# One more raw-weight buffer, one general slot and one residual slot fewer in a hybrid decoder layer

## The chip, the cores and the metric

The kernel runs on one core of one Trainium2 chip. The metric is the device time of one execution in microseconds (us), from launch to end. The span in the profile is a little shorter: it counts from the first to the last instruction.

## What is computed

One layer of a decoder trunk for 512 tokens of width 1024, in float32. Only the second half and the end of the first half matter for the change.

```python
u   = rms_norm(h, norm_mix_g)
z   = u @ w_in                                   # attention q/k/v, mLSTM inputs, gates ga, gb
m   = sigmoid(ga) * (ya @ w_proj_a) + sigmoid(gb) * (yb @ w_proj_b)
h   = h + m @ w_out                              # the first residual
u   = rms_norm(h, norm_ffn_g)
g, up = split(u @ w_gate_up)                     # 1024 x 5632
h   = h + (silu(g) * up) @ w_down                # 2816 x 1024, the second residual
out = rms_norm(h, norm_final_g)
```

Here `ya` is the output of a block-sparse attention and `yb` that of a chunkwise mLSTM; both are made from `z`.

## The kernel before

**Precision and weights.** TensorE takes operands in a float32 form of reduced precision. To keep the accuracy each operand is split into a high and a low half (`split_hl`, L157 to L162: ACT copies and rounds, DVE subtracts) and each product is three matmuls. So every weight tile passes through three places: a raw buffer that a DMA fills, ACT and DVE that split it, and two split tiles that PE reads.

**Buffers.** The pools are sized at L89 and L90. `NR` (tag R, 4 KB per partition) holds raw weights. `NW` (tag W, 4 KB, 10 of them) holds split halves and sums of weights. `NA` (tag A, 2 KB) holds everything general: activations, split halves of activations, gate tiles, outputs of a product on their way to DRAM. `NX` (tag X, 2 KB) holds the residual's input tiles `xr` and at the end the two tiles `g3` of the last norm's weights. `NR1` (tag R1) and `NA4` (tag A4) stay as they are. A tile takes a slot of its tag; the instruction that first writes it waits until the last reader of the slot's previous tile is done.

**Order.** Up to L1132 the order is written out by hand. Behind that a scheduler orders the instructions of each engine when the kernel is built, by priorities, by a model of times, and by slots that are free in that model; on the chip each engine and each queue takes its instructions in that fixed order. SP's queue carries nearly all loads; POOL's queue carries the accumulating DMAs.

**Front part (to some 404 us).** `UNITS` lists 60 weight tiles of 128 x 1024: q, k, va, ob, vb, qkb, ga, gb, then `p` (both projections) and `wo` (the output projection, eight units in the order `WO`). `load_pair` (L180) loads two raw tiles, `split_unit` (L189) splits them two units ahead of their use. Two tiles of the normalised input (`u`, L270) sit in the R pool as well, until the last unit that reads it, so this part has `NR` minus two raw buffers.

**Residual.** `load_xr` (L595) loads one tile of x on SP's queue: twice from `run_p`, then once in each `run_wo`. `run_wo` (L642) multiplies, adds the product into the `xr` tile (DVE, L651), and from the sum makes the operands `bq` of the gate-up products (L653 to L676). `residual` (L629) transposes the sum on PE (L635) one unit later and writes it to DRAM (`h1d`). An X slot is free when all of these have read it. `end_load` (L1063) puts `g3` into the same pool.

**Gate-up and down.** `ITEMS` lists 22 gate-up groups (`gu`), and after groups 4, 8, 12, 16 and 21 one down group (`ds`). Both use a Strassen-like scheme of seven products. `gu_load` (L688) loads for each group `w11` (R1) and two R tiles: `s13`, by a plain load on SP (L692) and an accumulating load on POOL (L693) that waits for the plain one, and `r` (L695). `ds_load` (L746) takes four R tiles (L750), the last one two more (L754). Loads are put in order with a look-ahead of three items (`load_next`, L1081). `gu_prep` (L722) makes sums and splits: S1 and S3 from `s13` (ACT L148, then DVE L731), S2 and S4 from `s24` (DVE L739, L740), and W12 and W22 from `r`. `gu_first`, `gu_main` and `gu_last` hold the products (`prod`, L777, whose three matmuls are L783 to L785); `ds_run` (L905) holds those of a down group (L894 to L896) and sends its results with accumulating DMAs on POOL's queue to `h1d` (L911).

Of the kernel before, what the change touches and what calls it, by code (L numbers as in the profile page):

```python
# [84 lines left out]
def hybrid_layer_kernel(ctx: ExitStack, tc, xT, wall, wgu, wds, wdl, g3v, vecs, wgates, consts, rope, out):  # L85
    nc = tc.nc
    V, A, T = nc.vector, nc.scalar, nc.tensor

    NA, NA4, NR, NR1, NW = 35, 7, 6, 3, 10  # L89
    NX = 3  # L90
    cst = ctx.enter_context(tc.tile_pool(name="cst", bufs=1))
    act = ctx.enter_context(tc.tile_pool(name="act", bufs=NA))
    sm = ctx.enter_context(tc.tile_pool(name="sm", bufs=6))
# [5 lines left out]
    def nm(p="t"):  # L99
        cnt[0] += 1  # L100
        return f"{p}{cnt[0]}"

    def slot(dt=F32, name="a"):
        return act.tile([P, S], dt, name=nm(name), tag="A")
# [490 lines left out]
    def load_xr():  # L595
        m = WO[len(xr)]
        t = act.tile([P, S], F32, name=nm("xr"), tag="X", bufs=NX)
        nc.sync.dma_start(t, xT[m])
# [464 lines left out]
    def end_load():  # L1063

        g3 = [act.tile([P, S], F32, name=nm("g3"), tag="X", bufs=NX) for _ in range(2)]
        hs = [[slot(name="h1") for _ in range(2)] for _ in range(4)]
# [519 lines left out]
```

## Time and profile before

| | us |
|---|---|
| median of 3 runs | 759.62 (758.28 to 760.0) |
| the profiled execution | 761.87 |
| its span | 760.1 |
| PE busy in it | 738.9 |
| DVE busy | 624.0 |
| ACT busy | 429.3 |
| DMA, mean over the span | 156 GB/s |

PE, TensorE's matmuls, is busy in 97% of the span; its weight loads run beside them. Matmuls overlap each other by their recorded durations, so the distance from one start to the next is the cost of one, not the duration in the row. The DMA engines' load is uneven: the page's slices go from 0 to over nine tenths and back in each period of the second part.

### The profile page before, as it was taken

The page shows a single profiled execution, that of the slowest core. Times are in us where ns is not written, and L with a number is a line of the kernel's source. Part 1 is how long each engine was busy: PE and PEld are TensorE (multiplying, and loading weights), DVE is VectorE, ACT ScalarE, POOL GpSimd, SP SyncE. Part 2 cuts the span into 40 slices and gives each one's busy share as a digit, 9 for nine tenths or more (in the row PEclk, how much of TensorE's full clock was granted, in tenths as well). Part 3 has the DMA queues.
Part 4 walks back from the last instruction along what each step waited for, and adds up shares of the span by engine and source line. Part 5 has one row for each costly group of instructions (what it writes and reads, how often), then busy time and mean ns, then how long its engine had stood idle before and what let it go on. Part 6 is the DMA issues. An engine that isn't in the chain of part 4 may idle for free. (4 is left out here: it accounts for less than half of the span.)

```text
span 760.1 us, 11421 instructions
## 1 busy us (share of the span) xinstructions
PE 738.9 (97%) x4230; PEld 639.0 (84%) x4230; DVE 624.0 (82%) x1065; ACT 429.3 (56%) x739; POOL 65.6 (9%) x82
## 2 busy tenths in 40 slices
PE   9998999999999999999999999989999999999994
PEld 5786888888888888888889997989899899899983
DVE  6896875889996787567688999878989988988996
ACT  7534666568765438523456566545745655665535
POOL 0002000000000000000000001300400400130003
PEclk9999999999999999999999999999999999999998
DMA  8776562432323213433676444962993795596402
GB/s 330 249 228 168 188 194 67 139 121 77 132 102 113 84 56 111 166 112 110 174 193 175 138 126 104 253 198 78 234 256 97 186 277 148 120 261 203 166 1 111
DMA packets 50839, 118.70 MB, mean 156 GB/s; under 512 B 4944, under 2 KB 9688, under 8 KB 50784
## 3 DMA queue, kind: packets, MB, share of 16 engines
q1 hardware_dynamic: 36832, 88.82, 34.7%
q0 software_dynamic: 9440, 26.77, 17.7%
q10 hardware_dynamic: 4512, 2.39, 1.0%
q8 instruction: 33, 0.54, 0.3%
q14 instruction: 22, 0.18, 0.1%
HBM read 101.16 MB, written 16.81 MB: 155 GB/s over the span
## 5 line engine op out<-in xcount | busy, mean ns | idle before, releaser
L148 ACT ACTIVATE wh<-raw 128x1024 fp32r<-128x1024 f32 x58 | 61.2, 1058 | 69.8 <-PE mm L202 63.0
L161 DVE TENSOR_TENSOR wl<-raw,wh 128x1024 fp32r<-128x1024 f32 x58 | 70.5, 1220 | 15.3 <-ACT wh L148 12.8
L783 PE MATMUL mm<-bq,w 128*128 128x256 f32 x264 | 77.0, 292 | 3.8 <-ACT s L148 3.3
L785 PE MATMUL mm<-bq,w 128*128 128x256 f32 x264 | 75.1, 284 | 0.0
L784 PE MATMUL mm<-bq,w 128*128 128x256 f32 x264 | 75.0, 284 | 0.0
L148 ACT ACTIVATE w<-s 128x1024 fp32r<-128x1024 f32 x44 | 46.6, 1060 | 45.7 <-DVE s L740 17.2
L731 DVE TENSOR_TENSOR w<-s,w 128x1024 fp32r<-128x1024 f32 x44 | 53.8, 1222 | 17.6 <-ACT w L148 15.8
L783 PEld LDWEIGHTS mm<-bq,w 128*128 128x128 f32 x264 | 50.7, 192 | 7.7 <-ACT s L148 5.4
L693 POOL DMA_DIRECT2D s<-in_wgu_dram x22 | 19.4, 882 | 413.8 <-DVE ga L585 127.8
L201 PE MATMUL mm<-u,wh 128*128 128x512 f32 x136 | 54.9, 403 | 0.0
L203 PE MATMUL mm<-u,wh 128*128 128x512 f32 x136 | 53.2, 391 | 0.0
L202 PE MATMUL mm<-u,wl 128*128 128x512 f32 x136 | 53.1, 390 | 0.0
L203 PE MATMUL mm<-ul,wh 128*128 128x512 f32 x136 | 52.9, 389 | 0.0
L201 PE MATMUL mm<-uh,wh 128*128 128x512 f32 x136 | 52.9, 389 | 0.0
L202 PE MATMUL mm<-uh,wl 128*128 128x512 f32 x136 | 52.9, 389 | 0.0
L148 ACT ACTIVATE w<-raw 128x1024 fp32r<-128x1024 f32 (+2 forms) x45 | 43.6, 974 | 15.4 <-PE s L784 9.2
L783 PE MATMUL s<-bq,w 128*128 128x256 f32 x176 | 50.3, 286 | 1.5 <-DVE gt L834 1.5
L784 PEld LDWEIGHTS mm<-bq,w 128*128 128x128 f32 x264 | 50.9, 193 | 0.1
L785 PEld LDWEIGHTS mm<-bq,w 128*128 128x128 f32 x264 | 50.9, 193 | 0.0
L785 PE MATMUL s<-bq,w 128*128 128x256 f32 x176 | 49.9, 283 | 0.0
L784 PE MATMUL s<-bq,w 128*128 128x256 f32 x176 | 49.7, 283 | 0.0
L148 ACT ACTIVATE w<-sw 128x1024 fp32r<-128x1024 f32 x20 | 21.2, 1060 | 31.2 <-DVE sw L770 29.4
(384 smaller groups left out, 2247.1 us busy)
## 6 DMA issues: line engine op xcount, KB each, us to landing
raw<-in_wall_dram SPq DMA_DIRECT2D x59, 512.0 KB, 3.4
s<-in_wgu_dram SPq DMA_DIRECT2D x22, 512.0 KB, 4.4
s<-in_wgu_dram POOLq DMA_DIRECT2D x22, 512.0 KB, 7.6
raw<-in_wgu_dram SPq DMA_DIRECT2D x22, 512.0 KB, 6.0
raw<-in_wds_dram SPq DMA_DIRECT2D x20, 512.0 KB, 7.1
w<-in_wgu_dram SPq DMA_DIRECT2D x22, 256.0 KB, 7.8
h1d<-s POOLq DMA_DIRECT2D x16, 256.0 KB, 12.4
R<-scr POOLq DMA_DIRECT2D x4, 896.0 KB, 4.8
```

The costliest lines, as they stand in the source:

```text
L148: return A.activation(out_, in_, func, **kw)
L161: V.tensor_tensor(l, src, f(h), op=ALU.subtract)
L201: T.matmul(ps, wh[:, c], rh[j], start=start and j == 0, stop=False)
L202: T.matmul(ps, wl[:, c], rh[j], start=False, stop=False)
L203: T.matmul(ps, wh[:, c], rl[j], start=False, stop=stop and j == n - 1)
L693: nc.gpsimd.dma_start(s13, wgu[i][:, 512:1536].rearrange("p (x c) -> p x c", x=2), accum_op=ALU.add)
L731: V.tensor_tensor(dst[1], src, f(dst[0]), op=ALU.subtract)
L783: T.matmul(ps, wh[:, c], bh, start=first and k == 0, stop=False, skip_group_check=not first)
L784: T.matmul(ps, wl[:, c], bh, start=False, stop=False, skip_group_check=not first)
L785: T.matmul(ps, wh[:, c], bl, start=False, stop=k == 3, skip_group_check=not first)
```

## The change

It changes three sizes: the R pool has seven buffers of 4 KB and not six, the A pool 34 slots of 2 KB and not 35, the X pool two slots of 2 KB and not three. The sum of the bytes is the same. No instruction is added or taken away. The scheduler may put instructions in another order, since the sizes are among its inputs.

```diff
--- before.py
+++ after.py
@@ -86,8 +86,8 @@
     nc = tc.nc
     V, A, T = nc.vector, nc.scalar, nc.tensor
 
-    NA, NA4, NR, NR1, NW = 35, 7, 6, 3, 10
-    NX = 3
+    NA, NA4, NR, NR1, NW = 34, 7, 7, 3, 10
+    NX = 2
     cst = ctx.enter_context(tc.tile_pool(name="cst", bufs=1))
     act = ctx.enter_context(tc.tile_pool(name="act", bufs=NA))
     sm = ctx.enter_context(tc.tile_pool(name="sm", bufs=6))
```

## Rows read from the trace of the kernel before

**Rows 1.** The first section of the page: busy time of each engine, its share of the span and the count of its instructions.

```profile
PE 738.9 (97%) x4230; PEld 639.0 (84%) x4230; DVE 624.0 (82%) x1065; ACT 429.3 (56%) x739; POOL 65.6 (9%) x82
```

**Rows 2.** The list of waits, for PE over the whole span: who waited, for whom, microseconds in total, times, the longest.

```profile
PE mm L783 <- ACT s L148: 3.3, 3, 2.1
...
PE s L783 <- DVE gt L834: 1.5, 3, 0.7
PE s L1219 <- DMA scr<-rr: 1.5, 1, 1.5
```

**Rows 3.** Busy time of each engine in stretches of 20 us: the stretch, its length, busy time of PE, weight loads, DVE, ACT and POOL with counts, granted clock of TensorE, share of the DMA engines, GB/s.

```profile
220.00:240.00 20.00, 20.00 (x97) 17.00 (x96) 13.59 (x25) 7.57 (x13) 0.54 (x1) 1.00 0.34 125
...
500.00:520.00 20.00, 17.92 (x135) 17.55 (x135) 15.00 (x28) 10.26 (x16) 0.88 (x1) 0.91 0.52 157
```

**Rows 4.** The timeline of PE, all its rows between 440 and 720 us that carry an idle time of over 0.2 us in front of a product of L783 (start, duration, engine, line, operation, tiles; in brackets the idle time before it and what ended it).

```profile
506.85 0.39 PE L783 MATMUL mm<-bq,w 128*128 128x256 f32 x1 [2.08 <-ACT s L148]
...
569.92 0.39 PE L783 MATMUL mm<-bq,w 128*128 128x256 f32 x1 [0.96 <-ACT s L148]
...
573.50 0.38 PE L783 MATMUL s<-bq,w 128*128 128x256 f32 x1 [0.45 <-DVE gt L834]
...
631.57 0.39 PE L783 MATMUL mm<-bq,w 128*128 128x256 f32 x1 [0.28 <-ACT s L148]
...
635.15 0.39 PE L783 MATMUL s<-bq,w 128*128 128x256 f32 x1 [0.45 <-DVE gt L834]
...
698.22 0.39 PE L783 MATMUL s<-bq,w 128*128 128x256 f32 x1 [0.65 <-DVE gt L834]
```

**Rows 5.** Busy time of PE, its instructions and the granted clock in two stretches right behind the idle time that ends at 506.85 us.

```profile
506.85:510.70 3.85, 3.85 (x19) 0.56 0.61 202
511.30:515.00 3.70, 3.70 (x33) 1.00 0.45 79
```

**Rows 6.** The timeline of ACT at the same four places; `w<-s` is the high half of a combination tile, `gt<-gt` the SiLU of the group before.

```profile
502.88 1.06 ACT L148 ACTIVATE w<-s 128x1024 fp32r<-128x1024 f32 x1 [4.04 <-DMA s<-in_wgu_dram]
505.90 0.63 ACT L153 ACTIVATE gt<-gt 128x512 f32<-128x512 f32 x1 [1.96 <-DVE gt L855]
...
565.94 1.06 ACT L148 ACTIVATE w<-s 128x1024 fp32r<-128x1024 f32 x1 [2.92 <-DMA s<-in_wgu_dram]
...
627.60 1.06 ACT L148 ACTIVATE w<-s 128x1024 fp32r<-128x1024 f32 x1 [2.24 <-DMA s<-in_wgu_dram]
...
688.94 1.06 ACT L148 ACTIVATE w<-s 128x1024 fp32r<-128x1024 f32 x1 [1.94 <-PE s L785]
```

**Rows 7.** The timeline of SP's queue: the moments at which loads into the 4 KB raw buffers were issued, in their order (`s` by L692 and `raw` by L695 are the two raw tiles of a gate-up group).

```profile
448.27 0.55 SPq L695 DMA_DIRECT2D raw<-in_wgu_dram  x1
465.28 0.38 SPq L692 DMA_DIRECT2D s<-in_wgu_dram  x1
...
473.58 0.55 SPq L695 DMA_DIRECT2D raw<-in_wgu_dram  x1
...
477.21 0.41 SPq L692 DMA_DIRECT2D s<-in_wgu_dram  x1
...
537.75 0.55 SPq L695 DMA_DIRECT2D raw<-in_wgu_dram  x1
...
541.38 0.44 SPq L692 DMA_DIRECT2D s<-in_wgu_dram  x1
...
600.11 0.55 SPq L695 DMA_DIRECT2D raw<-in_wgu_dram  x1
...
603.75 0.42 SPq L692 DMA_DIRECT2D s<-in_wgu_dram  x1
```

**Rows 8.** The timeline of POOL: the accumulating load into the `s` tile whose plain load was issued at 477.21 us.

```profile
490.23 0.88 POOL L693 DMA_DIRECT2D s<-in_wgu_dram  x1 [7.72 <-DMA s<-in_wgu_dram]
```

**Rows 9.** The columns of rows 3 in stretches of 5 us.

```profile
460.00:465.00 5.00, 5.00 (x32) 4.24 (x31) 3.70 (x7) 0.72 (x2) 0.00 (x0) 1.00 0.01 3
...
485.00:490.00 5.00, 5.00 (x44) 5.00 (x44) 3.74 (x6) 3.08 (x5) 0.00 (x0) 1.00 1.10 263
```

**Rows 10.** Four views about the residual's tiles: SP's issue of the first `xr` load that had to wait for a slot (the fourth of eight) and of the `g3` load that follows the eighth into the same pool; the line of L598's view with the shortest, median and longest time from issue to landing; DVE's additions into the third and the last `xr` tile and a split that follows; PE's first product that needs that split.

```profile
369.56 0.35 SPq L598 DMA_DIRECT2D xr<-in_xT_dram  x1
...
399.17 0.34 SPq L1068 DMA_DIRECT2D g<-in_g3v_dram  x1
...
DMA to landing us min/median/max: 2.7/5.0/7.1
...
375.03 0.69 DVE L651 TENSOR_TENSOR xr<-mm,xr 128x512 f32<-128x512 f32 x1 [0.31 <-PE mm L203]
...
404.97 0.69 DVE L651 TENSOR_TENSOR xr<-mm,xr 128x512 f32<-128x512 f32 x1
...
408.08 1.28 DVE L161 TENSOR_TENSOR bq<-v,bq 128x512 fp32r<-128x512 f32 x2
...
408.78 0.28 PE L783 MATMUL acc<-bq,w 128*128 128x256 f32 x1
```

**Rows 11.** DVE's longest wait between 235 and 245 us, and from the view of the tile `yb` PE's first reads of it and DVE's last writes to it (shortest, median and longest duration in ns, first and last start).

```profile
239.49 0.69 DVE L563 TENSOR_TENSOR ga<-mm,rn 128x512 f32<-128x512 f32 x1 [2.11 <-PE acc L1385]
...
L201 PE MATMUL mm<-yb,wh x32: 389/389/389, 317.2 to 357.3; 128*128 128x512 f32 x32
...
L161 DVE TENSOR_TENSOR yb<-nt,yb x4: 679/680/681, 296.9 to 301.7; 128x512 fp32r<-128x512 f32 x4
```

## Prediction

> **What bounds the kernel now.** I read the busy times first: PE is busy in 97% of the span, DVE in 82%, ACT in 56% [rows 1]. With no product added or removed, the change can only touch the 21 us in which PE stands still (760.1 - 738.9) and what follows from them. The list of PE's waits comes second: behind the start and the tail it names few causes, and in the second part they are two, a product of `gu_first` or `gu_main` that waits for ACT's copy `s12` (3.3 us in three places), and one that waits for DVE's sum of L834 (1.5 us in three) [rows 2]. The timeline of PE shows where: at 506.85, 569.92 with 573.50, 631.57 with 635.15, and 698.22 [rows 4]. That is one place per period of four gate-up groups and a down group, in the last group of the four. The first of them costs twice: behind its 2.08 us the granted clock is 0.56 for 3.85 us, most of it at the lower of the two levels, 1.2 GHz, and back at 1.00, 2.4 GHz, after that [rows 5]; the 20 us around it have the clock at 0.91 [rows 3].
>
> Third, what ACT did then. In each place it first waited for the tile `s13` of the next group, 4.04, 2.92 and 2.24 us, before it could make the high half of S1; the SiLU and the copy that PE needs stand behind that in ACT's fixed order, and DVE waits for the same half [rows 6]. The fourth place is different: there ACT waited 1.94 us for a product on PE (L785) which it doesn't read. That can only be the release of a W slot. So the fourth place shows what the same piece of order costs when the load is in time: 0.65 us of PE [rows 4, 6].
>
> Why is `s13` late? SP issued its plain load at 477.21, 3.63 us behind the raw load before it, and POOL's accumulating load could start only at 490.23, when the plain one had landed [rows 7, 8]; ACT went on at 502.88. So 25.7 us from the issue, in a stretch in which the DMA engines are full (share 1.10), while a few us earlier, from 460 to 465, they did nothing at all (0.01) [rows 9]: between 448.27 and 465.28 no R buffer came free [rows 7]. A buffer, not bandwidth, holds the loads back, and then they all come at once, together with the down group's stores.
>
> **The seventh R buffer.** Loads take buffers in the order of SP's queue. With one more, each load takes the release that its predecessor waits for now. For the three late tiles that is 477.21 to 473.58, 541.38 to 537.75 and 603.75 to 600.11, so 3.63, 3.63 and 3.64 us earlier [rows 7]. Besides, the load now issued at 465.28 moves to 448.27 or a little later, into the empty stretch; with its accumulating half it takes 2 x 0.52 MB, 4.0 us at the 263 GB/s of the full stretch, out of the queue ahead of the late tile [rows 7, 9]. I take the arrival as earlier by at least 3.6 us and at most 7.6. Against waits of 4.04, 2.92 and 2.24 the load then is no longer what comes last, or by 0.4 us in one place. What comes last next is the W slot, as in the fourth place. The sum:
>
> - idle time of PE that goes: 2.08 + 0.96 + 0.45 + 0.28 + 0.45 = 4.22 us [rows 4];
> - the low clock that goes with the 2.08 us: 3.85 x (1 - 0.56) = 1.69 us [rows 5];
> - what stays in these three places, sized by the fourth: 3 x 0.65 = 1.95 us [rows 4].
>
> 4.22 + 1.69 - 1.95 = 3.96 us gained. Its ends: if the load stays late by as much, 0; if the W slots also come earlier, so that all four places close, 4.22 + 1.69 + 0.65 = 6.56 us.
>
> In the front part the seventh buffer is a fifth one for raw weights. There ACT waits for W slots, not for loads, and PE doesn't stand still between 220 and 240 us, for one [rows 3]; I put this at nothing. One place is open: around 66 us PE waits 1.5 us for a DMA [rows 2], and a raw load that leaves this time for an earlier one could shorten that, by at most these 1.5 us, or lengthen it by as much if it comes in its way; I take nothing.
>
> **Two X slots instead of three.** Three `xr` loads are issued at the start; the fourth waits for a slot and goes at 369.56, and each later one about 6 us after that. With two slots the third `xr` tile takes the issue at 369.56, and so on, and the eighth takes that of the first `g3` load, 399.17 [rows 10]. The third is needed at 375.03, 5.47 us later, the eighth at 404.97, 5.80 us later; a load of this kind lands after 2.7 to 7.1 us, 5.0 in the median [rows 10]. In the median nothing is late. At 7.1 us the addition slips by 1.6 or 1.3 us. In the middle of the series that is hidden, since PE's transposes of the sum come one unit later; at the end it isn't: DVE's split of 408.08 is done with its first tile at about 408.77, and PE reads it at 408.78 [rows 10]. So the ends are 0 and 1.3 us; I take 0, since the median is nearer to the issue times. SP's queue has the same waits in the same places, for the same releases, so no other load is held up longer. The `g3` loads move back by one place each; nothing reads them before the tail.
>
> **34 general slots.** Where do the 35 bind? In the second part no wait of ACT or DVE ends with a store to `h1d`, whose landing is what frees the longest-held general slots there; I put that part at nothing. In the mLSTM stretch they do bind: at 239.49 DVE waits 2.11 us for a product (L1385) that its instruction, an evacuation into a fresh gate tile, doesn't read; it is a slot [rows 11]. With one slot less such waits become longer or more. They are covered twice: PE is busy 20.00 of 20 us there while DVE has 6.4 us left over [rows 3], and the end of that chain, `yb`, is written by 302.4 and first read at 317.2, 14.8 us later [rows 11]. I take 0; the bounds are 0 and 2.1 us, one wait of that length that reaches PE. A gain I exclude: a slot less releases nothing earlier.
>
> **Total.** 0 and 0 against 3.96. The profiled execution took 761.87 us with a span of 760.1, so it lies 2.25 us (0.3%) above the median; the places above are differences within it, and I take them off the median: 759.62 - 3.96 = 755.7 us.
>
> **Rivals.**
>
> *The load isn't what decides* (no change). At 631.57 and 635.15 the place costs 0.73 us with the load late by 2.24 us, at 698.22 it costs 0.65 with no load late [rows 4, 6]. If the W slot comes nearly as late as the load in the other places too, only parts of 2.08 and 1.69 us go; or the freed buffer is given to another load, and the late one stays late behind the stores in POOL's queue. For it: W slots already decide one place of four. Against it: the other three are ended by a DMA. A gain of 0 to 1.5 us, so some 758.9 us. Chance 0.22.
>
> A sentence on the notes stands here by itself: the Trainium skill, "DMA: Bandwidth & Descriptors", section "Anatomy of one DMA", gives a fixed 2.0 us and bytes over 436 GB/s for a DMA, which would make an estimated 3.2 us of each half of `s13`; by that rule both halves would be there long before 502.88, a seventh buffer would gain nothing and the time would stay at 759.6. The trace disagrees: the accumulating half alone took from 490.23 to 502.88 [rows 6, 8], so I leave that rule no chance of its own.
>
> *The W slots take over, and more* (slower). With raw weights there sooner, the scheduler lets ACT and DVE run ahead with the splits of the down group; these take W slots, and the high half of S1 that PE's order hangs on gets its slot one product later. A product is twelve matmuls, 0.112 us each by the full-clock stretch (3.70 / 33) [rows 5], so 1.35 us. In the four places that makes 4 x (0.65 + 1.35) = 8.0 us of idle time in place of 4.22 + 0.65 + 1.69 = 6.56, so 761.1 us; and if two of these waits also bring the low clock, 1.69 us each, 764.4. It decides from the point where ACT's wait of 1.94 us at 688.94 becomes over 2.9 us: 4 x (0.65 + 0.99) = 6.56 [rows 6]. Against it: priorities follow due times, and the down group's are later. Chance 0.15, and with it 0.05 that the last `xr` load (1.3 us) or a general slot (2.1 us) takes more than the buffers give back.
>
> *More than expected.* All four places close, and the wait at 66 us shortens: 6.56 + 1.5 = 8.1 us, 751.5 us. Chance 0.08.
>
> *The change doesn't do what it says* can't be: the pools' sizes are what the loads wait for.
>
> **How the numbers follow.** The forecast has 0.50, with its own range from 753.1 (6.56 us) to 758.0 (3.96 - 1.3 - 1.0 for half of a general slot's wait). The range from 752.6 to 761.5 leaves out half of the last rival and the part of the slower one that brings the low clock. A measurement of this kernel tells 0.2%, 1.5 us, from no change. Faster by more than that: the forecast and the last rival, 0.58. Slower: most of the slower cases, 0.17. The rest is 0.25.
>
> **What would show it.** Right: ACT's waits for `s13` at the three places are gone or under 0.5 us; loads are issued between 450 and 465 us; the clock stays at 1.00 around 507; PE's idle time in the last group of each four is 0.65 us or less. Wrong: ACT's waits there become waits for PE's products of 2.9 us or more; PE waits at 408.8 for the last `xr`; the evacuations around 240 us stand long enough that PE waits for a PSUM tile.

## The result, and the profile after

The changed kernel takes 754.58 us (median of 6 runs, 753.11 to 755.75), the kernel before in the same session 759.44 us (6 runs, 758.28 to 763.28). The ratio is 0.9922 with a 95% interval of 0.9902 to 0.9941: faster by 0.8%. The forecast was 755.7 in a range of 752.6 to 761.5. The profiled execution took 755.75 us with a span of 754.0, 6.1 us less than the one before.

Its list of waits for PE (columns as in rows 2), down to 0.3 us; there are no more:

```profile
PE mm L470 <- DVE va L487: 1.6, 1, 1.6
PE s L1219 <- DMA scr<-rr: 1.3, 1, 1.3
PE s L217 <- DVE zero L214: 1.2, 1, 1.2
PE mm L894 <- DVE h L975: 1.0, 1, 1.0
PE mm L894 <- ACT s L148: 0.5, 1, 0.5
PE mm L201 <- DVE ga L563: 0.3, 1, 0.3
```

Both causes of the second part [rows 2] have left the list, and so all four places of [rows 4] are closed, the fourth too. The last line is new. ACT's timeline at the four places answers to [rows 6]:

```profile
501.45 1.06 ACT L148 ACTIVATE w<-s 128x1024 fp32r<-128x1024 f32 x1 [0.50 <-ACT s L148]
...
561.78 1.06 ACT L148 ACTIVATE w<-s 128x1024 fp32r<-128x1024 f32 x1 [0.49 <-ACT s L148]
...
622.15 1.06 ACT L148 ACTIVATE w<-s 128x1024 fp32r<-128x1024 f32 x1 [0.49 <-ACT s L148]
...
682.56 1.06 ACT L148 ACTIVATE w<-s 128x1024 fp32r<-128x1024 f32 x1 [0.50 <-ACT s L148]
```

Where ACT waited 4.04, 2.92, 2.24 and 1.94 us it now waits 0.5 us, and not for a load. SP's queue answers to [rows 7], POOL's timeline to [rows 8]:

```profile
450.35 0.38 SPq L692 DMA_DIRECT2D s<-in_wgu_dram  x1
467.36 0.55 SPq L695 DMA_DIRECT2D raw<-in_wgu_dram  x1
467.95 0.59 SPq L692 DMA_DIRECT2D s<-in_wgu_dram  x1
471.51 0.55 SPq L695 DMA_DIRECT2D raw<-in_wgu_dram  x1
475.66 0.37 SPq L692 DMA_DIRECT2D s<-in_wgu_dram  x1
...
484.77 0.88 POOL L693 DMA_DIRECT2D s<-in_wgu_dram  x1 [4.27 <-DMA s<-in_wgu_dram]
```

The load that stood at 465.28 is issued at 450.35, in the stretch that had been empty. The late one leaves at 475.66, and since PE is 2.1 us later at this point than before (table below), that is 3.6 us earlier against the work, as worked out. Its accumulating half starts at 484.77, not at 490.23. The DMA view of 484 to 486 us gives that half 9.5 us from issue to landing (tile, queue, operation, size, us):

```profile
s<-in_wgu_dram POOLq DMA_DIRECT2D x1, 512.0 KB, 9.5
```

So the tile is there at 494.3, 7.2 us before ACT takes it up at 501.45.

Where the time went is read best from the starts of the same matmul in two traces, counted by line (the n-th of a line). Microseconds, the changed kernel less the one before; differences are of the unrounded starts, and the last column tells where each is made:

```
matmul                     before    after   difference   gained (-) or lost since the row above
L201, the 100th            151.84   152.87      +1.03      +1.03   start and recurrent part
L201, the 240th            280.72   282.79      +2.07      +1.04   general slots
L783, the 197th            498.86   500.96      +2.10      +0.03   residual's tiles, up to the first place
L783, the 589th            708.51   702.37      -6.14      -8.24   the four places
L894, the 140th            749.44   743.31      -6.12      +0.02   tail
```

The stretches of 20 us show the rows behind it (columns as in rows 3):

```profile
220.00:240.00 20.00, 19.72 (x94) 16.42 (x93) 13.47 (x25) 6.42 (x12) 0.54 (x1) 1.00 0.36 124
240.00:260.00 20.00, 19.87 (x95) 16.49 (x94) 16.24 (x27) 10.43 (x17) 0.00 (x0) 1.00 0.27 91
260.00:280.00 20.00, 19.94 (x93) 16.19 (x93) 14.90 (x22) 8.19 (x13) 0.00 (x0) 1.00 0.19 66
500.00:520.00 20.00, 20.00 (x160) 19.58 (x160) 18.77 (x34) 11.71 (x19) 1.76 (x2) 1.00 0.66 180
60.00:80.00 20.00, 17.15 (x69) 13.04 (x68) 12.16 (x25) 8.84 (x18) 1.52 (x3) 0.83 0.56 162
```

At 500 us PE is busy in 20.00 of 20 us and the clock is at 1.00 [rows 3]. At 220 us, where it had been busy for 20.00 us, 0.28 are missing now and 0.13 in the next stretch; from 260 to 280 us 0.06 are missing, and 0.04 were before. And from 60 to 80 us the clock was 0.83.

### The profile page after: what moved, and what is told of

The parts are those of the page before. It is cut to its first block, busy times and chain, and to the rows that moved or that the text cites. A ratio compares the mean times of both kernels' runs of the same rounds, so it can differ in the third digit from the quotient of the medians.

```text
span 754.0 us, 11434 instructions
## 1 busy us (share of the span) xinstructions
PE 737.6 (98%) x4230; PEld 638.5 (85%) x4230; DVE 624.4 (83%) x1065; ACT 430.6 (57%) x739; POOL 65.8 (9%) x82
## 4 chain that ended last, share of the span: by engine, by line
PE 90%; DVE 5%; DMA 2%; ACT 1%; issue 1%; SPq 0%; DVEq 0%; ACTq 0%
PE mm L201 12%; PE mm L202 12%; PE mm L203 12%; PE mm L783 6%; PE mm L785 6%; PE mm L784 6%; PE s L783 3%; PE s L785 3%; PE s L784 3%; PE mm L894 3%; PE mm L896 2%; PE mm L895 2%; PE acc L1309 1%; PE acc L783 1%; PE acc L784 1%; PE acc L785 1%
## 5 line engine op out<-in xcount | busy, mean ns | idle before, releaser
L783 PE MATMUL mm<-bq,w 128*128 128x256 f32 x264 | 76.1, 288 | 0.4
L785 PE MATMUL mm<-bq,w 128*128 128x256 f32 x264 | 74.7, 283 | 0.0
L201 PE MATMUL mm<-u,wh 128*128 128x512 f32 x136 | 55.1, 405 | 0.3 <-DVE ga L563 0.3
L693 POOL DMA_DIRECT2D s<-in_wgu_dram x22 | 19.4, 880 | 395.6 <-DVE ga L585 123.5
L783 PEld LDWEIGHTS mm<-bq,w 128*128 128x128 f32 x264 | 50.6, 191 | 3.2 <-ACT x L148 1.9
L201 PE MATMUL mm<-uh,wh 128*128 128x512 f32 x136 | 52.9, 389 | 0.0
L785 PEld LDWEIGHTS mm<-bq,w 128*128 128x128 f32 x264 | 50.6, 192 | 0.0
L783 PE MATMUL s<-bq,w 128*128 128x256 f32 x176 | 50.2, 285 | 0.0
L785 PE MATMUL s<-bq,w 128*128 128x256 f32 x176 | 49.9, 283 | 0.0
```

Source lines behind the costliest of these rows:

```text
L201: T.matmul(ps, wh[:, c], rh[j], start=start and j == 0, stop=False)
L693: nc.gpsimd.dma_start(s13, wgu[i][:, 512:1536].rearrange("p (x c) -> p x c", x=2), accum_op=ALU.add)
L783: T.matmul(ps, wh[:, c], bh, start=first and k == 0, stop=False, skip_group_check=not first)
L785: T.matmul(ps, wh[:, c], bl, start=False, stop=k == 3, skip_group_check=not first)
```

## The experiments

Theory: the accumulating load of `s13` came too late in every fourth group; the seventh buffer brings it earlier, and a general slot is the price. Rivals: the general or the X slots matter, the operand slots (W) matter, or the order that the scheduler makes around the buffers does. In each edit below the lines shown replace lines 89 and 90 of the kernel before (`NA, NA4, NR, NR1, NW = 35, 7, 6, 3, 10` and `NX = 3`), unless it says otherwise. "Places" is the difference to the kernel before made between the 197th and the 589th matmul of L783, "slots" that between the 100th and the 240th of L201, both as in the table above.

**The price without the buffer.**

```diff
+    NA, NA4, NR, NR1, NW = 34, 7, 6, 3, 10
+    NX = 2
```

> Six raw buffers, but 34 general and two residual slots: the price alone. Between 217 and 280 us the changed kernel's matmuls fell back by 1.0 us against those of before, in a stretch where general slots are all in use. If the general slot is the cause, this kernel falls back by about 1.0 us there too, keeps the four stalls of the gate-up groups and takes 760.0 to 761.0 us. If that loss came from the other order that the raw buffers make, it takes the same time as before within 0.3 us. The residual slots should cost nothing in either case: no idle time of PE near 408.8 us.

Measured: 762.13 us (12 runs), ratio 1.0011 (0.9989 to 1.0033). Slots +0.88, places -0.24. PE's waits:

```profile
PE mm L783 <- ACT s L148: 3.5, 4, 1.1
PE s L783 <- DVE gt L834: 2.0, 4, 0.7
```

With six buffers the places stay, now with four waits of each kind, and ACT's timeline has a wait for the load in all four:

```profile
503.62 1.06 ACT L148 ACTIVATE w<-s 128x1024 fp32r<-128x1024 f32 x1 [3.03 <-DMA s<-in_wgu_dram]
...
566.31 1.06 ACT L148 ACTIVATE w<-s 128x1024 fp32r<-128x1024 f32 x1 [2.97 <-DMA s<-in_wgu_dram]
...
628.81 1.06 ACT L148 ACTIVATE w<-s 128x1024 fp32r<-128x1024 f32 x1 [3.08 <-DMA s<-in_wgu_dram]
...
690.44 1.06 ACT L148 ACTIVATE w<-s 128x1024 fp32r<-128x1024 f32 x1 [2.21 <-DMA s<-in_wgu_dram]
```

So the fourth place, which I had given to a W slot, waits for a load here like the others.

**The same memory given to operand slots.**

```diff
+    NA, NA4, NR, NR1, NW = 34, 7, 6, 3, 11
+    NX = 2
```

> The same price as the change, but the 4 KB go to an eleventh slot for split weights and not to a raw buffer. If late raw loads are the cause of the stalls (my theory), ACT still waits for s13 by DMA in three places, by 2 to 4 us, and only the fourth place, which was a split slot's, may close: 759 to 761 us. If split slots were the real limit (the rival), all four places close: 753 to 756 us.

Measured: 777.57 us (4 runs), ratio 1.0227 (1.0190 to 1.0264). Neither theory had this. ACT waits for no load of `s13` any more, but PE has a new wait at the start of each down group, 12.9 us in four. PE's timeline at the first:

```profile
470.86 0.38 PE L783 MATMUL s<-bq,w 128*128 128x256 f32 x1 [3.94 <-ACT w L148]
471.43 0.71 PE L894 MATMUL mm<-w,ach 128*128 128x512 f32 x1 [0.19 <-ACT s L148]
```

and ACT's in front of it:

```profile
466.82 1.06 ACT L148 ACTIVATE w<-sw 128x1024 fp32r<-128x1024 f32 x1 [2.64 <-DVE sw L770]
467.78 0.61 ACT L148 ACTIVATE ach<-up 128x512 fp32r<-128x512 f32 x1
468.30 1.04 ACT L148 ACTIVATE w<-raw 128x1024 fp32r<-128x1024 f32 x1
469.25 0.61 ACT L148 ACTIVATE w11h<-w 128x512 fp32r<-128x512 f32 x1
469.77 1.04 ACT L148 ACTIVATE w<-s 128x1024 fp32r<-128x1024 f32 x1
470.71 1.24 ACT L148 ACTIVATE s<-mm,rc 128x512 f32<-128x512 f32 x2
```

With an eleventh slot the order written for PE puts one matmul of the next gate-up group (L783) ahead of the down group's products (L894). Its operand `w<-s` is split at 469.77, behind operands of the down group; the evacuation `s<-mm` stands behind that too. PE stands still for 3.94 us, and the granted clock is 0.59 from 470.86 to 474.90 us, most of it at the lower level of 1.2 GHz, and 1.00 from 475.20 on. In the kernel before, with ten slots, the products of L894 come directly behind the W11 product, at 468.16 with 0.46 us of idle time. That this order is the cause is read from the rows; no further run tested it.

**The buffer with more of the price, and with less of the other.**

```diff
+    NA, NA4, NR, NR1, NW = 33, 7, 7, 3, 10
+    NX = 3
```

> Seven raw buffers, paid with two general slots; three residual slots as before. My theory: the four stalls are closed as in the changed kernel, 8 us less in the second part; between 217 and 280 us two slots fewer cost 1 to 4 us in place of 1.0: 754.5 to 758 us. If the residual's two slots had cost something hidden, this kernel would be faster than the changed one.

Measured: 756.52 us (12 runs), ratio 0.9941 (0.9918 to 0.9963). Places -8.32, all closed; slots +3.12. The second missing slot costs about twice as much as the first.

```diff
+    NA, NA4, NR, NR1, NW = 35, 7, 7, 3, 10
+    NX = 1
```

> Seven raw buffers, 35 general slots, and one residual slot. My theory: the four stalls are closed and nothing is lost between 217 and 280 us, but each residual tile is loaded only when the one before has been transposed, some 5 us before it lands; in the middle the transposes come one unit later and hide it, at the end PE waits about 5 us near 408 us, with 1.7 us of low clock at times: 757 to 761 us. If the residual slots don't matter, 753 us.

Measured: 764.24 us (12 runs), ratio 1.0057 (1.0036 to 1.0077). Places -8.24, slots +0.04. One X slot costs 3.29 us up to the 28th matmul of L783 (415.94 us in the kernel before), where PE waits for the last residual tiles, and 4.16 up to the 197th. The tail costs more, which I had not thought of: the second `g3` tile shares the slot with the first, and from the last product of L894 to the end of the span it takes 17.5 us in place of 10.7. PE's timeline, then DVE's and POOL's:

```profile
409.43 0.66 PE L635 MATMUL s<-con,xr 128*128 128x128 f32 x4 [1.25 <-DVE xr L651]
...
754.02 2.42 DVE L1000 SCALAR_TENSOR_TENSOR h<-h,v,g 128x512 f32<-128x512 f32 x2 [3.73 <-DMA g<-in_g3v_dram]
...
754.13 3.43 POOL L985 TENSOR_TENSOR h<-h,g 128x512 f32<-128x512 f32 x2 [15.12 <-DMA g<-in_g3v_dram]
```

**The load made smaller, nothing else moved.** Line 693 of the kernel before. Every engine keeps its order of instructions, so only the transfer changes:

```diff
-        nc.gpsimd.dma_start(s13, wgu[i][:, 512:1536].rearrange("p (x c) -> p x c", x=2), accum_op=ALU.add)
+        nc.gpsimd.dma_start(s13[:, :, 0:64], wgu[i][:, 512:1536].rearrange("p (x c) -> p x c", x=2)[:, :, 0:64], accum_op=ALU.add)
```

> Six raw buffers, all slots as before, the same order of instructions on every engine. Left out: of every accumulating load that makes `s13` (w11 + w21 and w13 + w23 in one tile) only the first 64 of 512 columns are added, so an eighth of its bytes is moved; the matmuls run on the incomplete sums. Theory (the load's arrival is what stood in the way in three places): the plain load is still issued near 477, since the buffers come free as before, but the accumulating one lands some 3 us instead of 12.6 us after its issue, so ACT's waits for s13 by DMA (4.04, 2.92, 2.24 us) are gone. The W slots and the order are as before, so the fourth place keeps its 0.65 us, and the three others keep at most as much: 4.22 + 1.69 of idle time and clock, and 0.26 us per stall that its row doesn't show, less 3 x 0.65: about 4 to 5 us faster, 755.5 to 756.5. Rival (it is the earlier release of buffers and slots, and the order planned around it, not the transfer): ACT's waits turn from DMA to slots, the three places stay, 760.5. Second rival (the load was also what held the fourth place): all four places close, 752.5 to 753.

Measured: 753.40 us (6 runs), ratio 0.9900 (0.9877 to 0.9923). Places -8.30, everything else within 0.2 us of the kernel before: the second rival, all four places. Its view of L693 has the time from issue to landing (shortest, median, longest):

```profile
DMA to landing us min/median/max: 2.9/4.3/8.8
```

Before they were 5.3, 7.6 and 12.6 us. ACT at the fourth place:

```profile
680.55 1.06 ACT L148 ACTIVATE w<-s 128x1024 fp32r<-128x1024 f32 x1 [0.50 <-ACT s L148]
```

With six buffers, ten W slots and the old order the wait of 1.94 us is 0.50. A W slot held nothing there. In the trace of before, POOL issues the accumulating load of this group's `s13` at 678.57 us, and the DMA view of 678 to 679.5 us says how long it took:

```profile
s<-in_wgu_dram POOLq DMA_DIRECT2D x1, 512.0 KB, 10.3
```

678.57 + 10.3 = 688.87, and ACT went on at 688.94 [rows 6]. In the other three places the same view gives 12.6, 12.0 and 10.7 us, so landings at 502.83, 565.84 and 627.52, and ACT went on at 502.88, 565.94 and 627.60: four times within 0.1 us of the landing. The matmul of L785 that the fourth row names only ended at nearly the same moment.

**The smaller load in the changed kernel**, with the changed sizes.

> The changed kernel, with an eighth of the bytes in each accumulating load that makes `s13` (only 64 of 512 columns are added; the matmuls run on incomplete sums). Theory (in the changed kernel no load of a gate-up group ends a wait any more): no difference from the changed kernel, 754.6. Rival (the loads still cost it something that its rows of idle time don't name): 753 or less.

Measured: 754.79 us (6 runs), ratio 0.9911 (0.9887 to 0.9935), with the changed kernel at 754.92 beside it; places -8.35. With seven buffers the smaller load brings nothing: both remedies cure one and the same lateness.

**The parts of the price by themselves.**

```diff
+    NA, NA4, NR, NR1, NW = 34, 7, 6, 3, 10
+    NX = 3
```

> One general slot less and nothing else: six raw buffers, three X slots. Theory: 1.0 us is lost between 217 and 280 us, where both kernels with 34 slots lose it, and nothing elsewhere; the four places stay: 761.5. Rival (the slot is free, and the 1.0 us belongs to the X slots or to the changed order): 760.5, no difference at the same matmul at 281 us.

Measured: 760.54 us (12 runs), ratio 0.9999 (0.9982 to 1.0015). Slots +1.18, as the theory has it; places -2.11: in the profiled execution the loads were less late (ACT's longest wait is 3.3 us, not 4.04), and the clock is 1.00 from 500 to 520 us. The time alone couldn't have told theory and rival apart.

```diff
+    NA, NA4, NR, NR1, NW = 35, 7, 6, 3, 10
+    NX = 2
```

> Two X slots instead of three and nothing else. Theory: nothing is lost near 409 us, the four places stay, 760.5. Rival (the moved loads of the residual or of the third gates' tiles get in the way of the raw loads): the four places move by up to 1.5 us in all, one way or the other, or PE waits near 409 us for up to 1.3 us.

Measured: 759.86 us (12 runs), ratio 0.9984 (0.9963 to 1.0006). Slots +0.04, around 409 us 0.00, places -2.53 with ACT's four waits for the load at 2.73 us or less. Two X slots cost nothing. Whether the moved loads make the four places a little cheaper, or this execution only drew shorter ones, stays open.

**More buffers still, and other ways to pay.**

```diff
+    NA, NA4, NR, NR1, NW = 32, 7, 8, 3, 10
+    NX = 2
```

> Eight raw buffers, two X slots, 32 general slots. Theory (seven buffers already take the loads off the path, and a general slot costs more the fewer there are: 1.0 us for one, 3.1 us for two): the four places stay closed and nothing more is gained in the second part; between 150 and 281 us three missing slots cost 4.5 to 6 us, so 758 to 760. Rival (the loads are still partly late, and the eighth buffer brings the front part's loads forward too): the price is paid back by 1 to 3 us, 755 to 757.

Measured: 758.87 us (12 runs), ratio 0.9976 (0.9962 to 0.9989). Places -8.03, slots +4.25 for three. An eighth buffer gains nothing.

```diff
+    NA, NA4, NR, NR1, NW = 35, 7, 7, 2, 10
+    NX = 2
```

> Seven raw buffers and two X slots as in the change, but 35 general slots, paid for with one of the three 2 KB buffers for `w11`. Theory (the general slot costs the change 1.0 us between 217 and 280 us, the rest of the change is gain): the four places stay closed, nothing is lost between 217 and 280, so 1.0 us under the changed kernel: 753.5. Rival (SP's queue now waits for a `w11` buffer ahead of the load of `s13`, so the late load is late again): ACT waits for s13 or PE for W11's halves in the second part, 0.7 us or more in each of four places, 757 or more. Second rival (that 1.0 us came from the order and not from the slot): 754.6.

Measured: 760.06 us (12 runs, 755.20 to 765.18), ratio 0.9987 (0.9965 to 1.0009). Slots +0.03, the late `s13` is cured, but places only -4.29: the load of `w11` is late now, in another group of the four. ACT at one of these points:

```profile
607.63 0.63 ACT L148 ACTIVATE w11h<-w 128x512 fp32r<-128x512 f32 x1 [2.85 <-DMA w<-in_wgu_dram]
```

PE waits 1.45 us at 608.59 for what stands behind it. The rival has the mechanism, a late load again, but not its place.

**The price paid elsewhere.** The changed kernel with 35 general slots; two constant tiles give the 2 KB.

```diff
-    NA, NA4, NR, NR1, NW = 34, 7, 7, 3, 10
+    NA, NA4, NR, NR1, NW = 35, 7, 7, 3, 10
-    zero = cst.tile([P, S], BF16, name="zero")
+    zero = act.tile([P, S], F32, name="zero", tag="A").bitcast(BF16)[:, 0:S]
-    ones = cst.tile([P, P], F32, name="ones")
-    V.memset(ones, 1.0)
+    one = act.tile([P, S], F32, name="one", tag="A")[:, 0:P]
+    V.memset(one, 1.0)
-    V.tensor_copy(onesr, ones)
+    V.tensor_copy(onesr, one); ones = f(onesr)
```

> Seven raw buffers, two X slots, and 35 general slots: the 2 KB come from two constant tiles, the zeros of the warm-up matmuls and the plain ones, which take a general slot for a short while at the start (the ones are read from the rounded copy after that). Theory (the lost general slot is the price in the changed kernel, 1.0 to 1.2 us between 217 and 280 us): the four places stay closed, nothing is lost there, so 1.0 us under the changed kernel run beside it: 753.5. Rival (the price belongs to the order that the scheduler makes, not to the slot): no difference from the changed kernel.

> The changed kernel itself, to stand beside the others of this batch: 754.6, a ratio of 0.992 to the kernel before.

Measured: 753.77 us (6 runs), ratio 0.9904 (0.9879 to 0.9930); the changed kernel beside it 754.92 us (6 runs), 0.9920 (0.9897 to 0.9944). Places -8.36 and -8.35; slots +0.03 here and +1.20 in the changed kernel. The stretches of the version with 35 slots:

```profile
220.00:240.00 20.00, 20.00 (x101) 17.11 (x100) 13.62 (x25) 8.53 (x16) 0.54 (x1) 1.00 0.30 106
```

PE is at 20.00 of 20 us again. The two intervals overlap, so the times alone don't show it; the difference of the medians, 1.15 us, is near what the slots column says, 1.17. The run shows that the price goes with the 35th slot and not with the order made around seven buffers. It doesn't part the slot from the order that the scheduler makes with 34 (next section).

## Why the prediction was right, step by step

- **What bounds the kernel**: right. Nothing but PE's standstill in the four places changed for the better.
- **The load of `s13` is late for want of a buffer**: right for three places, and right for the fourth, which I had ruled out. The sentence "That can only be the release of a W slot" is the step that failed. The row named a product that ACT doesn't read, and I took it for a slot; the load issued at 678.57 landed about 0.1 us before ACT went on, and with a smaller load alone 0.50 of the 1.94 us is left. With it falls "What comes last next is the W slot".
- **Earlier by 3.6 to 7.6 us**: too little. The accumulating half lands at 494.3; before, ACT went on at 502.88. That is 8.6 us by the clock, and 10.7 with the 2.1 us by which PE was later. The issue gave 3.6 of it, as forecast; from there to POOL's start it took 9.1 us (475.66 to 484.77) in place of 13.0 [rows 7, 8], and the accumulating half 9.5 in place of 12.6. For what the moved load takes out of the late one's way I had allowed at most 4.0 us; these two differences, 3.9 and 3.1, make 7.0.
- **What stays, 3 x 0.65 = 1.95 us**: nothing stayed, and the fourth place's 0.65 went as well. I had worked out this end myself (6.56 us), and given it to a rival at 0.08 only.
- **4.22 us of idle time**: too low by what the rows of idle time leave out. Around one stall, PE's timeline of before:

```profile
568.68 0.28 PE L785 MATMUL acc<-bq,w 128*128 128x256 f32 x1
569.92 0.39 PE L783 MATMUL mm<-bq,w 128*128 128x256 f32 x1 [0.96 <-ACT s L148]
570.14 0.28 PE L784 MATMUL mm<-bq,w 128*128 128x256 f32 x1
570.26 0.28 PE L785 MATMUL mm<-bq,w 128*128 128x256 f32 x1
```

  Matmuls start 0.12 us apart here and each row lasts 0.28, so they overlap. Idle time is counted from the end of the last row; from start to start the stall takes 1.24 us in place of 0.12, and the next start comes 0.22 behind, not 0.12. That is 1.22 us for a row of 0.96, 0.26 more. Six such rows: 1.56 us. 4.22 + 0.65 + 1.69 + 1.56 = 8.12, against the 8.24 measured. The Trainium skill, "Perfetto Trace Analysis", section "Tensor Engine Instruction (MATMUL, LD_WEIGHTS)", says that the end of a matmul in a profile is computed and not observed. No run here shows how the ends are made; the rows show that they lie behind the next starts.
- **The low clock, 1.69 us**: right for that execution, but not a part of every one. In three six-buffer kernels (the price without the buffer, 34 general slots, two X slots) the clock from 500 to 520 us is 1.00, and against a place-free run their four places cost 8.36 - 0.24 = 8.1, 6.2 and 5.8 us.
- **34 general slots at nothing**: wrong, within its bounds of 0 and 2.1 us. One slot costs 0.88 to 1.20 us in five runs (2.63 with the eleventh operand slot, whose order is another), two cost 3.12, three 4.25; with 35 slots it is 0.04 or less. The cover I named (DVE's slack, `yb` early) was beside the point: a gate's evacuation that comes late holds the PSUM tile of PE's next product; hence the new line "PE mm L201 <- DVE ga L563". I had named that sign under what would show me wrong. But the evacuation is not late by a longer wait for a slot, as I had pictured it; it has another place in DVE's order. The kernel before, then the changed one:

```profile
227.33 0.68 DVE L563 TENSOR_TENSOR ga<-mm,rn 128x512 f32<-128x512 f32 x1
231.21 1.14 DVE L1340 SCALAR_TENSOR_TENSOR R<-con,cS,R 128x128 f32<-128x128 f32 x4 [1.95 <-DMA R<-scr]
...
233.18 1.14 DVE L1340 SCALAR_TENSOR_TENSOR R<-con,cS,R 128x128 f32<-128x128 f32 x4 [2.45 <-DMA R<-scr]
234.23 0.68 DVE L563 TENSOR_TENSOR ga<-mm,rn 128x512 f32<-128x512 f32 x1
...
234.97 0.50 PE L201 MATMUL mm<-u,wh 128*128 128x512 f32 x1 [0.28 <-DVE ga L563]
```

  With 35 slots the scheduler puts the evacuation ahead of L1340, which waits for a DMA. With 34 it stands behind L1340, in all five runs with 34 slots and ten operand slots. At this product 0.58 of the 1.04 us arise, and 0.39 at the first one of L1405, whose operand DVE splits later than before (247.68, not 244.70). So the slot count costs, since 34 general slots alone bring it about, and by these rows it does so by way of an order. Whether a slot would have been free earlier on the chip, no run tells.
- **Two X slots at nothing**: right; one slot would have cost 4.16 us and a late tail.
- **The front part**: the stretch up to the 100th matmul of L201, with the place near 66 us in it, moved by +1.03 us here and by -0.09 us in another execution of the same kernel. That is within the ±1.5 us I had left open, and no effect of the change. In the three traces whose clock over 60 to 80 us is 1.00 (one X slot, two X slots alone, seven buffers with 35 slots) it is -1.06, -1.34 and -1.53 us; but the clock isn't all of it, since the price without the buffer has +0.82 with 0.91, the same clock as before.

So 3.96 us were forecast, and by the medians 4.86 came of it (759.44 - 754.58; 5.89 in the later runs, 760.81 - 754.92). Between the two traces the four places gave 8.24, the general slot took 1.04, and the front part of this execution 1.03. The traced execution of before lies 2.25 us above the median of the runs made with it, so 8.24 is more than the usual gain: by the medians the smaller load alone is worth 7.47 us (760.87 - 753.40), and seven buffers with 35 slots 7.04 (760.81 - 753.77). A gain and a price, both sized too low, met near the middle; that the total came so near is luck. The rival "W slots take over" didn't come about with seven buffers. An eleventh operand slot did slow the kernel, by 2.3%, as far as the rows show by way of an order nobody had asked for.

The Trainium skill, "Perfetto Trace Analysis", section "Optimization Strategy", reads the same gap repeating on the engine that should be saturated as a possible sign of too little SBUF or PSUM for the next tile, to be sought in buffer count and tile sizes. The runs agree in part: one more buffer closed the gaps for -8.2 us, but a load of an eighth of the bytes closed them with the old buffers, and an operand slot more in place of the buffer made the kernel slower.

## What to carry to other kernels

Before you call a wait a slot's, add the landing time of the loads in flight to their issue: a releaser that the waiting instruction doesn't read is a coincidence until a time says otherwise. Count a stall from start to start of the instructions, not from the idle time in its row. And when memory is moved between pools, look for the payer that nothing waits for (constants, the spare residual slots), since one general slot here ate an eighth of what the buffer gained. Where a scheduler plans with the pools' sizes, compare the orders too: here a size cost time by moving an instruction.

## What the runs showed of the hardware that was not expected

- The same accumulating load of 512 KB took from 5.3 to 12.6 us within one execution. At the first place ACT waited for it for 4.04, 3.03, 3.25 and 2.73 us in four kernels with six buffers and ten operand slots.
- Near 66 us the granted clock differs between executions of one kernel: over 60 to 80 us it was 0.83 in the first profile of the changed kernel and 0.91 in its second. The second:

```profile
60.00:80.00 20.00, 17.04 (x74) 13.09 (x73) 13.38 (x27) 9.59 (x19) 1.65 (x4) 0.91 0.59 166
```

  What decides it in one execution stays open.
